# Input laid out by numpy: x and the output transposed, parameter vectors as columns, w_ada summed along rows

## The chip, the cores and the metric

The kernel runs on one core of a Trainium2 chip. TensorE (PE in the profile) multiplies matrices; VectorE (DVE), ScalarE (ACT) and GpSimd (POOL) do the elementwise work; SyncE (SP) issues most of the transfers, and a second queue is ScalarE's. The measure is the time of one execution on the device in microseconds, as a median of several runs.

## The reference

x is 512 tokens of 1024 features; 16 meta tokens are put in front, so 528 tokens pass through the first block. It has two layers, then a norm; the second block has one layer whose norms are modulated by a vector c.

```python
for l in range(2):                       # first block
    u = rms_norm(h, ln_mix[l])
    (aq, ..., gz) = split_in(u @ w_in[l])
    y_a = windowed_sink_attention(...)   # y_b: axial rope, y_c: differential, y_d: gated linear attention
    merged = sum(gate[n] * (y_n @ w_branch[l, n]))
    h = h + merged @ w_out[l]
    u = rms_norm(h, ln_ffn[l])
    h = h + (silu(u @ w_ffn_gate[l]) * (u @ w_ffn_up[l])) @ w_ffn_down[l]
x = rms_norm(h, ln_final)[:, META_END:]

mod = silu(c) @ w_ada + b_ada            # second block: 1024 -> 9 x 1024
sh1, sc1, ga1, sh2, sc2, ga2, sh3, sc3, ga3 = split(mod, 9)
h = rms_norm(x, g_pre_ff1) * (1 + sc1) + sh1
x = x + 0.5 * ga1 * rms_norm(swiglu(h, ...), g_post_ff1)
# mixer: sliding-window attention and a state space model, with sh2, sc2, ga2
# a second swiglu with sh3, sc3, ga3
```

## The kernel before

The activations stay transposed in SBUF: eight tiles h[k] of 128 features by 528 tokens. Every product is in fp32 precision made of three matmuls of rounded operands (mm3, L258 to L260): high by high, low by high, high by low. A weight tile arrives through SP's queue in a raw tile `wr` (L215, L217), ScalarE rounds it to its high half (L218), VectorE subtracts for the low half (L219). The tokens are worked on in two halves, (0, 272) and (272, 528), or without the meta tokens (16, 272) and (272, 528).

A norm squares the tiles on ScalarE (L86), sums the squares over the features by matmuls against a column of ones (L97, one per 128 tokens and tile), computes the reciprocal root on VectorE (L107, L268 to L275), spreads it over the partitions by TensorE (L112, L115), copies that as a row to SBUF (L116, L117), and scales and splits the tiles (L345, L230, L231).

load_x (L363) brings x in as four tiles of 128 tokens by 1024 features, transposes the 128x128 blocks on TensorE (L376, L387), copies them from PSUM on VectorE (L378, L388), and stores the tiles to `hd` in DRAM (L357), from where the end of the layer reads the old h again (L353). columns (L303) brings parameter vectors as rows into a `stage` tile with a transfer each on ScalarE's queue (L311, L315), transposes them (L321) and copies them as columns (L323). ada (L1834) is called 72 times in between other work: for 128 outputs it loads two pieces of w_ada of 128x4x128 (L1840) into `ho`, a pool of two tiles, adds up the eight products with c on VectorE (L1844, L1846), sums over the partitions by a matmul with ones (L1848), and adds b_ada (L1849). The last norm of the second block scales (L2238) and adds the old x (L2241); out (L2613) then transposes each half to tokens by features (L2623), copies it from PSUM (L2624), and stores it (L2626).

A class Plan at the end of the file takes all instructions and draws an order for every engine, SP's queue among them, by a list scheduler with costs and priorities, and fixes it by dependencies. So the text of the program doesn't give the order, and any change in the work draws a new one for all engines.

Of the kernel before, what the change touches and what calls it, by code (L numbers as in the profile page):

```python
# [119 lines left out]
class Net:  # L120
# [35 lines left out]
    def small(self, w, tag, bufs=None):  # L156
        self.n += 1
        if w > 32:
            return self.sp.tile([P, 128], F32, tag="wide", name=f"{tag}_{self.n}", bufs=2)[:, :w]
        if w > 8:  # L160
            return self.sp.tile([P, 32], F32, tag="mid", name=f"{tag}_{self.n}", bufs=6)[:, :w]
        return self.sp.tile([P, 8], F32, tag="tiny", name=f"{tag}_{self.n}", bufs=56)[:, :w]
# [115 lines left out]
    def setup(self):  # L278
        nc, cp, I = self.nc, self.cp, self.ins
        o = self.offs["rest"][0]  # L280
        self.misc = cp.tile([P, self.offs["total"][0]], F32, tag="misc", name="misc")
# [3 lines left out]
        self.hd = self.dp.tile([KC, P, NT], F32, tag="hd", name="hd")  # L285
        self.lo_engs = [nc.vector]
# [6 lines left out]
    def setup_rest(self):  # L293
        nc, I = self.nc, self.ins
        o = self.offs["rest"][0]
        nc.scalar.dma_start(self.misc[:, o:], I["c_misc"][:, o:])
# [5 lines left out]
    def columns(self, groups):  # L302

        nc = self.nc
        rows, where = 0, {}
        st = self.small(P, "stage", bufs=2)
        for keys, ap, wide in groups:
            nl = len(keys)
            if wide:
                n = ap.shape[1] // P  # L310
                nc.scalar.dma_start(st[rows:rows + nl * n, :], ap.rearrange("l (a b) -> (l a) b", b=P))  # L311
            else:
                n = 1
                for s in range(2):
                    nc.scalar.dma_start(st[rows:rows + nl, 64 * s:64 * s + 64], ap)  # L315
            for k in keys:
                where[k] = (rows, n)
                rows += n
        self.n += 1
        ps = self.pst("t")  # L320
        nc.tensor.transpose(ps[:, :rows], st[:rows, :], self.ident[:rows, :rows])  # L321
        col = self.cp.tile([P, rows], F32, tag=f"col{self.n}", name=f"col{self.n}")
        nc.vector.tensor_copy(col, ps[:, :rows])  # L323
        self.col.update({k: col[:, r:r + n] for k, (r, n) in where.items()})
# [38 lines left out]
    def load_x(self):  # L363
        nc, I = self.nc, self.ins
        with self.pool("xin", "R") as xp:
            mt = xp.tile([NM, 1024], F32, name="mt")
            nc.scalar.dma_start(mt, I["meta_tokens"])
# [3 lines left out]
            self.columns([([f"ln_mix{l}" for l in range(2)], I["ln_mix"], True)])  # L371
            self.ahead = [self.wload(w, KC) for w in self.qk_columns(0, 512)]
            self.h = [self.xtile("hn") for _ in range(KC)]
            pm = self.pst("t")
            for k in range(KC):
                nc.tensor.transpose(pm[:, k * NM:(k + 1) * NM], mt[:, k * P:(k + 1) * P], self.ident[:NM, :NM])  # L376
            for k in range(KC):
                nc.vector.tensor_copy(self.h[k][:, 0:NM], pm[:, k * NM:(k + 1) * NM])  # L378
            sq = self.squares()
            norm = None  # L380
            for i, (a, b) in enumerate(self.halves(0)):
                for k in range(0, KC, 2):
                    ps = self.pst("mm")
                    for j in range(2):
                        for t in range(2):
                            o = (2 * j + t) * P
                            nc.tensor.transpose(ps[:, o:o + P], xt[2 * i + t][:, (k + j) * P:(k + j + 1) * P], self.ident)  # L387
                        nc.vector.tensor_copy(self.h[k + j][:, NM + 256 * i:b], ps[:, 256 * j:256 * j + 256])  # L388
                        sq.add(self.h[k + j], a, b)
                norm = norm or self.norm(sq, self.h, self.col["ln_mix0"], 0)  # L390
                norm(i)
            for k in range(KC):
                self.store_h(k, 0)
# [75 lines left out]
    def params1(self):  # L469
        nc, I = self.nc, self.ins  # L470
        cp = self.cp
        two = lambda n: [f"{n}{l}" for l in range(2)]
        self.columns([(two("ln_ffn"), I["ln_ffn"], True), (["ln_final"], I["ln_final"][None, :], True)] + self.params2_names())
        g = [(["b_ada"], I["b_ada_2"], True)] if "b_ada_2" in I else []
        self.columns(g + [(two("qn"), I["qk_norm_q"], False), (two("kn"), I["qk_norm_k"], False),
                          (two("sub"), I["diff_subnorm"], False), (two("hout"), I["hgrn_out_norm"], False)])
        self.sink, self.sinkM, self.nlam = [], [], []
        self.gq = []
        for l in range(2):
# [8 lines left out]
            d = self.small(128, "lam", bufs=2)  # L488
            nc.scalar.dma_start(d, I["diff_lambda"][l:l + 1].rearrange("a b c -> a (b c)").to_broadcast([P, 128]))
            dv = d.rearrange("p (a b c) -> p a b c", a=2, b=2)  # L490
            pr = self.small(64, "lamp", bufs=2)
# [85 lines left out]

# [1216 lines left out]


CM = 3


class Parts:

# [1294 lines left out]
```

## Time and profile before

| | us |
|---|---|
| median of 3 runs | 3288.27 |
| lowest, highest | 3285.03, 3296.5 |
| profiled execution | 3297.02 |
| its span in the trace | 3295.2 |
| TensorE busy | 3096.8 (94%) |
| TensorE weight loads busy | 2717.5 (82%) |
| VectorE busy | 1857.9 (56%) |
| ScalarE busy | 1277.6 (39%) |
| GpSimd busy | 418.2 (13%) |

The mean granted clock of TensorE was 0.962 of full speed. The profile lists, for the engines by line, how long they were busy and what ended their idle time; a weight load (PEld) runs beside the matmul before it. A line number is that of the kernel; a helper's line gathers the work of all its callers.

### The profile page before, as it was taken

To read this page: it belongs to the slowest core of one execution; us is meant where nothing else is said; L and a number is where in the kernel's file an instruction comes from. 1 tells how busy PE (TensorE), PEld (TensorE's weight loads), DVE (VectorE), ACT (ScalarE), POOL (GpSimd) and SP (SyncE) were. 2 spreads that over 40 slices of the span, in tenths; PEclk is the share of its full clock that TensorE was granted. 3 is DMA by queue.
4 is the path that set the end of the run, shared out by engine and by line. 5 is a ranking of instruction groups with operands and counts; after the bars stand their busy time and mean duration, and the time that the engine had idled before them with its cause. 6 is when DMAs were issued, how large, how long until landed. Compare 5 with 4: busy or idle time off the path is not lost. (4 is left out here: it accounts for less than half of the span.)

```text
span 3295.2 us, 57803 instructions
## 1 busy us (share of the span) xinstructions
PE 3096.8 (94%) x21892; PEld 2717.5 (82%) x21892; DVE 1857.9 (56%) x5063; ACT 1277.6 (39%) x2856; POOL 418.2 (13%) x444
## 2 busy tenths in 40 slices
PE   7888999999999978899999999999999998899997
PEld 6777888999999977777678878789888987888887
DVE  4466588744645857567975464864222655732224
ACT  2356444333232245564434322243232535433332
POOL 1101000002110011020001111421110111211101
PEclk9899999999999988899999999989999999889998
DMA  4721223343544673022344354574333565133342
GB/s 139 178 51 45 73 73 95 103 126 112 157 122 120 172 169 67 27 79 81 93 134 142 112 150 133 166 222 121 93 96 111 147 187 152 53 109 96 92 124 93
DMA packets 645883, 380.41 MB, mean 115 GB/s; under 512 B 66500, under 2 KB 613884, under 8 KB 645476
## 3 DMA queue, kind: packets, MB, share of 16 engines
q1 hardware_dynamic: 628520, 365.22, 38.0%
q0 software_dynamic: 13632, 9.61, 2.0%
q8 instruction: 172, 2.82, 0.4%
q10 hardware_dynamic: 3452, 1.89, 0.2%
q14 instruction: 107, 0.88, 0.1%
HBM read 333.16 MB, written 45.52 MB: 115 GB/s over the span
## 5 line engine op out<-in xcount | busy, mean ns | idle before, releaser
L258 PE MATMUL ps_mm<-u,wh 128*128 128x256 f32 (+2 forms) x2928 | 970.8, 333 | 19.6 <-ACT g L1514 4.2
L260 PE MATMUL ps_mm<-u,wh 128*128 128x256 f32 (+2 forms) x2928 | 961.9, 330 | 0.3 <-DVE u L231 0.2
L259 PE MATMUL ps_mm<-u,wh 128*128 128x256 f32 (+2 forms) x2912 | 955.9, 330 | 4.6 <-DVE wh L219 4.6
L258 PEld LDWEIGHTS ps_mm<-u,wh 128*128 128x128 f32 x2928 | 563.1, 193 | 77.3 <-issue 12.0
L218 ACT ACTIVATE wh<-wr 128x512 fp32r<-128x512 f32 (+1 forms) x588 | 354.5, 619 | 690.9 <-PE ps_mm L259 261.7
L219 DVE TENSOR_TENSOR wh<-wr,wh 128x512 fp32r<-128x512 f32 (+1 forms) x531 | 367.5, 704 | 450.1 <-issue 231.3
L259 PEld LDWEIGHTS ps_mm<-u,wh 128*128 128x128 f32 x2912 | 560.3, 193 | 53.3 <-DVE wh L219 5.5
L260 PEld LDWEIGHTS ps_mm<-u,wh 128*128 128x128 f32 x2928 | 562.1, 193 | 50.9 <-issue 4.7
L259 PE MATMUL ps_mm<-hid,wh 128*128 128x256 f32 (+2 forms) x988 | 299.1, 311 | 3.4 <-DVE wh L219 3.4
L258 PE MATMUL ps_mm<-hid,wh 128*128 128x256 f32 (+2 forms) x948 | 287.7, 312 | 2.7 <-ACT wh L218 2.7
L260 PE MATMUL ps_mm<-hid,wh 128*128 128x256 f32 (+2 forms) x948 | 287.4, 311 | 0.0
L1846 DVE SCALAR_TENSOR_TENSOR acc<-ho,cact,acc 128x128 f32<-128x128 f32 x504 | 186.6, 374 | 40.0 <-DMA ho<-in_w_ada_dram 32.5
L259 PEld LDWEIGHTS ps_mm<-hid,wh 128*128 128x128 f32 x988 | 185.1, 191 | 15.8 <-DVE wh L219 4.6
L258 PEld LDWEIGHTS ps_mm<-hid,wh 128*128 128x128 f32 x948 | 178.0, 191 | 13.2 <-ACT wh L218 2.9
L260 PEld LDWEIGHTS ps_mm<-hid,wh 128*128 128x128 f32 x948 | 178.0, 191 | 9.7 <-issue 0.4
L231 POOL TENSOR_TENSOR hid<-g,hid 128x512 fp32r<-128x512 f32 (+1 forms) x85 | 92.4, 1087 | 684.6 <-ACT hid L230 684.6
L218 ACT ACTIVATE wh<-wrx 128x512 fp32r<-128x512 f32 (+1 forms) x160 | 96.0, 601 | 205.5 <-PE ps_mm L260 100.6
L219 DVE TENSOR_TENSOR wh<-wrx,wh 128x512 fp32r<-128x512 f32 (+1 forms) x131 | 87.4, 668 | 136.5 <-issue 115.8
L88 POOL TENSOR_TENSOR na<-na,g 128x256 f32<-128x256 f32 (+2 forms) x62 | 63.4, 1022 | 771.6 <-issue 418.2
L258 PE MATMUL ps_mm<-u,hid 128*128 128x256 f32 (+1 forms) x448 | 133.3, 298 | 16.1 <-ACT hid L218 16.0
L259 PE MATMUL ps_mm<-u,hid 128*128 128x256 f32 (+1 forms) x448 | 133.6, 298 | 5.2 <-DVE hid L219 5.1
L260 PE MATMUL ps_mm<-u,hid 128*128 128x256 f32 (+1 forms) x448 | 132.5, 296 | 0.0
(591 smaller groups left out, 5575.9 us busy)
## 6 DMA issues: line engine op xcount, KB each, us to landing
wr<-in_w_in_dram SPq DMA_DIRECT2D x220, 256.0 KB
ho<-in_w_ada_dram SPq DMA_DIRECT2D x144, 256.0 KB
wr<-in_w_ffn_down_dram SPq DMA_DIRECT2D x80, 256.0 KB
wr<-in_w_down_dram SPq DMA_DIRECT2D x66, 256.0 KB
wr<-in_w_ffn_gate_dram SPq DMA_DIRECT2D x62, 256.0 KB
wr<-in_w_gate_dram SPq DMA_DIRECT2D x61, 256.0 KB
wr<-in_w_ffn_up_dram SPq DMA_DIRECT2D x60, 256.0 KB
wr<-in_w_up_dram SPq DMA_DIRECT2D x60, 256.0 KB
```

The costliest lines, as they stand in the source:

```text
L88: nc.gpsimd.tensor_tensor(out=acc[:, a:b], in0=acc[:, a:b], in1=sq[:, a:b], op=ALU.add)
L218: self.last_split = nc.scalar.activation(hi[:, i:e], raw, AF.Copy)
L219: (nc.vector if o else eng).tensor_tensor(out=lo[:, i:e], in0=raw, in1=hi[:, i:e].bitcast(F32), op=ALU.subtract)
L231: (eng or self.nc.vector).tensor_tensor(out=lo, in0=x, in1=hi.bitcast(F32), op=ALU.subtract)
L258: T.matmul(o, lhsT=wh, rhs=xh[:, a:b], start=start, stop=False)
L259: T.matmul(o, lhsT=wl, rhs=xh[:, a:b], start=False, stop=False)
L260: T.matmul(o, lhsT=wh, rhs=xl[:, a:b], start=False, stop=stop)
L1846: V.scalar_tensor_tensor(out=acc, in0=w[:, k], scalar=c, in1=acc, op0=ALU.mult, op1=ALU.add)
```

## The change

The sizes of the work on activations and the weight matrices' loads are untouched. Numpy hands over some inputs in another order, before the launch, and turns the output after it.

```diff
 def load_x(self):
-    xt = [xp.tile([P, 1024], F32, tag="xt", name=f"xt{b}", bufs=4) for b in range(4)]
-    for b in range(4):
-        nc.sync.dma_start(xt[b], I["x"][0, b * P:(b + 1) * P, :])
...
-                    nc.tensor.transpose(ps[:, o:o + P], xt[2 * i + t][:, (k + j) * P:(k + j + 1) * P], self.ident)
-                nc.vector.tensor_copy(self.h[k + j][:, NM + 256 * i:b], ps[:, 256 * j:256 * j + 256])
...
-    for k in range(KC):
-        self.store_h(k, 0)
+    self.columns(True)
+    for a, b in self.halves(0):
+        for k in range(KC):
+            nc.sync.dma_start(self.h[k][:, a:b], I["c_x"][k][:, a:b])
+        if a == 0:
+            self.ahead = [self.wload(w, KC) for w in self.qk_columns(0, 512)]
...
 def old_h(self, f, a, b=NT):
-    self.nc.sync.dma_start(t[:, a:b], self.hd[f][:, a:b])
+    self.nc.sync.dma_start(t[:, a:b], self.hsrc[f][:, a:b])
...
 def columns(self, first):
+    self.nc.scalar.dma_start(self.cols[:, t], ap[:, t])
...
 def ada(self, g):
-    ws = [self.xtile("ho")[:, :512].rearrange("p (k f) -> p k f", k=4) for _ in range(2)]
...
-                V.scalar_tensor_tensor(out=acc, in0=w[:, k], scalar=c, in1=acc, op0=ALU.mult, op1=ALU.add)
-    nc.tensor.matmul(ps[:, 0:1], lhsT=acc, rhs=self.ones[:, 0:1], start=True, stop=True)
-    V.tensor_tensor(out=self.mod[:, g:g + 1], in0=ps[:, 0:1], in1=self.col["b_ada"][:, g:g + 1], op=ALU.add)
+    for e in range(2):
+        w = self.xtile("ho")[:, :512]
+        self.nc.sync.dma_start(w, self.ins["c_ada"][g, e])
+        self.nc.vector.tensor_tensor_reduce(out=w, in0=w, in1=self.cact, scale=1.0, scalar=0.0, op0=ALU.mult, op1=ALU.add,
+                                            accum_out=self.mod[:, 72 * e + g:72 * e + g + 1])
...
 def ada_end(self):
+        self.nc.sync.dma_start(b, self.ins["c_bada"][:, 24 * i:24 * i + 24])
+        for e in range(2):
+            self.nc.tensor.matmul(ps[64 * e:64 * e + 64, :24], lhsT=self.const("fold"),
+                                  rhs=self.mod[:, 72 * e + 24 * i:72 * e + 24 * i + 24],
+                                  start=True, stop=True, tile_position=(0, 64 * e), skip_group_check=True)
+        V.tensor_tensor(out=m, in0=ps[:, :24], in1=b, op=ALU.add)
...
 def half(n):
-                    nc.tensor.transpose(ps[:, k * P:(k + 1) * P], f[4 * i + k][:, a + b * P:a + (b + 1) * P], self.ident)
-                (nc.vector.tensor_copy if i else nc.scalar.copy)(o[:, :512], ps)
-                nc.sync.dma_start(self.outs["out"][0][t:t + P, 512 * i:512 * (i + 1)], o[:, :512])
+            nc.sync.dma_start(self.outs["out"][k][:, 256 * n:256 * n + 256], f[k][:, a:a + 256])
...
-    mk = self.misc[:, o + QOFF[m]:o + QOFF[m] + n2]
+    mk = self.qmask[:, QOFF[m]:QOFF[m] + n2]
...
+def laid_out(inputs):
+    tokens = np.concatenate([a["meta_tokens"], a["x"][0]], 0)
+    return {"c_x": tokens.T.reshape(KC, P, NT), "c_cols": np.concatenate([columns_of(a, n, w) for n, w in VECTORS], 1),
+            "c_bada": columns_of(a, "b_ada_2", False),
+            "c_ada": a["w_ada_2"][0].T.reshape(72, 2, 64, 2, 512).transpose(0, 1, 3, 2, 4).reshape(72, 2, P, 512)}
```

old_h reads c_x until the first layer's new h is stored, and `hd` from then on; columns is called twice, with one load each. The lines with `mk` are masked_q's; the rope's `perm` is handled alike, and SP loads both tables once a layer. In c_ada one output's 1024 weights stand along two rows of 512 on partitions p and p + 64, so a piece has 64 outputs; c, made silu on ScalarE and VectorE, is spread over the partitions as 128x512, and the `fold` matmuls add the two partitions of an output. The pool tag "wide" is gone, "tiny" has 52 tiles for 56.

The planner's order moves at the places where work goes. TensorE at the start, before: transposes of the second half (L387, `xt`) and the sums of its squares (L97) stand among the first products (L258, L259).

```order
L387 MATMUL ps_mm_344<-misc,xt_86 128x128
L258 MATMUL ps_mm_586<-u_225,wh_97 128x272
L259 MATMUL ps_mm_586<-u_225,wh_98 128x272
L97 MATMUL ps_q_304<-misc,g_310 128x1 x2
L387 MATMUL ps_mm_344<-misc,xt_85 128x128
L387 MATMUL ps_mm_344<-misc,xt_86 128x128
L97 MATMUL ps_q_304<-misc,g_318 128x1 x2
```

The third matmul of the first product comes only after more transposes and sums, eleven rows on.

TensorE at the start, in the changed kernel: the sums of the first half (L97), the broadcast (L112, L115), and the first products (L256 to L258).

```order
L97 MATMUL ps_q_156<-misc,g_190 128x1 x3
L112 MATMUL ps_t_214<-misc,nr_198 128x128 x2
L115 MATMUL ps_t_214<-misc,nr_198 128x16
L256 MATMUL ps_mm_470<-u_138,wh_96 128x272
L257 MATMUL ps_mm_470<-u_138,wh_97 128x272
L258 MATMUL ps_mm_470<-u_139,wh_96 128x272
L256 MATMUL ps_mm_470<-u_140,wh_96 128x272
```

The transposes are gone from it, and the first products follow the broadcast at once.

TensorE at the end, before: the last product of the first half (L258 to L260 with `ps_mm_34674`), the sums (L97), the broadcast (L112), the transposes of the output (L2623, nine of them in a row), and then the second half's products.

```order
L258 MATMUL ps_mm_34674<-hid_33851,wh_34664 128x256
L259 MATMUL ps_mm_34674<-hid_33851,wh_34665 128x256
L260 MATMUL ps_mm_34674<-hid_33852,wh_34664 128x256
L97 MATMUL ps_q_34745<-misc,na_31883 128x1 x2
L97 MATMUL ps_q_34745<-misc,g_34743 128x1 x2
L112 MATMUL ps_t_34769<-misc,nr_34753 128x128 x2
L2623 MATMUL ps_mm_34790<-misc,hn_34029 128x128
L2623 MATMUL ps_mm_34790<-misc,hn_34129 128x128
```

The second half's first product (`ps_mm_34821`) comes behind the last of these transposes.

TensorE at the end, in the changed kernel: the sums (L97) and then products of the second half (`ps_mm_34090`). The broadcast (L112) stands 66 matmuls later.

```order
L256 MATMUL ps_mm_33989<-hid_33043,wh_33856 128x256
L257 MATMUL ps_mm_33989<-hid_33043,wh_33857 128x256
L258 MATMUL ps_mm_33989<-hid_33044,wh_33856 128x256
L97 MATMUL ps_q_33937<-misc,na_31075 128x1 x2
L97 MATMUL ps_q_33937<-misc,g_33935 128x1 x2
L256 MATMUL ps_mm_34090<-hid_31076,wh_34060 128x256
L257 MATMUL ps_mm_34090<-hid_31076,wh_34061 128x256
L258 MATMUL ps_mm_34090<-hid_31077,wh_34060 128x256
```

The broadcast, which needs VectorE's result, no longer stands right behind the sums.

SP's queue in the first layer's last part, before: pieces of w_ada (L1840, `ho`) between weight loads (L217, `wr`).

```order
L217 DMA wr_19310<-in_w_branch_dram 128x2x128
L1840 DMA ho_18796<-in_w_ada_dram 128x4x128
L1840 DMA ho_18797<-in_w_ada_dram 128x4x128
L217 DMA wr_19316<-in_w_in_dram 128x4x128
L217 DMA wr_19320<-in_w_in_dram 128x4x128
L217 DMA wr_19410<-in_w_branch_dram 128x2x128
L1840 DMA ho_19032<-in_w_ada_dram 128x4x128
L217 DMA wr_19416<-in_w_in_dram 128x4x128
L217 DMA wr_19420<-in_w_in_dram 128x4x128
L1840 DMA ho_19033<-in_w_ada_dram 128x4x128
L217 DMA wr_19531<-in_w_branch_dram 128x2x128
```

One or two pieces stand between two or three weight loads here.

SP's queue about there, in the changed kernel: the pieces (L1827) stand in runs, between weight loads (L215) and the load of the mask table (L1181).

```order
L1827 DMA ho_17884<-in_c_ada_dram 128x512
L215 DMA wr_17550<-in_w_in_dram 128x4x128
L215 DMA wr_17623<-in_w_branch_dram 128x2x128
L1827 DMA ho_17887<-in_c_ada_dram 128x512
L1827 DMA ho_18095<-in_c_ada_dram 128x512
L1827 DMA ho_18098<-in_c_ada_dram 128x512
L1827 DMA ho_18290<-in_c_ada_dram 128x512
L1827 DMA ho_18293<-in_c_ada_dram 128x512
L215 DMA wr_17629<-in_w_in_dram 128x4x128
L1181 DMA qmask<-in_c_qmask_dram 128x62
L215 DMA wr_17633<-in_w_in_dram 128x4x128
L215 DMA wr_17729<-in_w_branch_dram 128x2x128
```

Five pieces now stand in a row before the next weight load.

Over the whole queue, three or more pieces of w_ada stand in a row at 26 places (16 runs of three, 7 of four, 3 of five), where before it was 4 (1 of three, 2 of four, 1 of five). On TensorE 17609 rows of the order become 17472, on VectorE 4783 become 4561, on ScalarE 2654 become 2642, and on SP 1454 become 1471.

## Rows read from the trace of the kernel before

**Rows 1.** The page: busy us, share and instructions of each engine.

```profile
PE 3096.8 (94%) x21892; PEld 2717.5 (82%) x21892; DVE 1857.9 (56%) x5063; ACT 1277.6 (39%) x2856; POOL 418.2 (13%) x444
```

**Rows 2.** Forty slices, two of them: busy us (instructions), granted clock, DMA share, GB/s.

```profile
411.90:494.30 82.40, 82.17 (x994) 73.94 (x996) 67.57 (x145) 37.95 (x102) 5.11 (x10) 1.00 0.25 73
...
1977.10:2059.50 82.40, 82.40 (x367) 67.12 (x366) 37.50 (x83) 20.54 (x36) 11.03 (x8) 1.00 0.45 133
```

**Rows 3.** Timeline of the start: start us, us, engine, line, operation, count, [idle before].

```profile
7.56 6.16 SPq L215 DMA_DIRECT2D wr<-in_w_in_dram  x8
...
23.43 0.16 DVE L107 TENSOR_SCALAR nv<-ps_q 128x3 f32<-128x3 f32 x1 [5.76 <-PE ps_q L97]
...
23.58 0.61 ACT L218 ACTIVATE wh<-wr 128x512 fp32r<-128x512 f32 x1
...
27.56 0.16 DVE L275 SCALAR_TENSOR_TENSOR nr<-rt,ry 128x3 f32<-128x3 f32 x1
...
29.39 0.38 ACT L117 COPY g<-ps_t 128x256 f32<-128x256 f32 x1
...
37.75 0.57 PE L258 MATMUL ps_mm<-u,wh 128*128 128x272 f32 x1
...
39.51 5.12 PE L97 MATMUL ps_q<-misc,g 128*128 128x1 f32 x24
...
44.49 0.57 PE L260 MATMUL ps_mm<-u,wh 128*128 128x272 f32 x1
```

**Rows 4.** Slices of 5 us at the start.

```profile
5.00:10.00 5.00, 1.73 (x11) 1.32 (x11) 0.86 (x8) 0.72 (x1) 0.00 (x0) 1.00 1.05 319
```

**Rows 5.** Timeline of TensorE at one of the w_ada sums.

```profile
2052.47 0.39 PE L259 MATMUL ps_mm<-u,wh 128*128 128x512 f32 x1
2052.70 0.39 PE L260 MATMUL ps_mm<-u,wh 128*128 128x512 f32 x1
2052.92 0.28 PE L1848 MATMUL ps_t<-misc,acc 128*128 128x1 f32 x2
...
2053.38 0.39 PE L259 MATMUL ps_mm<-u,wh 128*128 128x512 f32 x1
```

**Rows 6.** Line L1846: who waited for it (us, times).

```profile
  PE ps_t L1848: 6.4, 8
```

**Rows 7.** Costliest groups of the page: busy us, mean ns, idle before, releaser.

```profile
L1846 DVE SCALAR_TENSOR_TENSOR acc<-ho,cact,acc 128x128 f32<-128x128 f32 x504 | 186.6, 374 | 40.0 <-DMA ho<-in_w_ada_dram 32.5
```

**Rows 8.** Lines L1335 and L1096 on VectorE: ns min/median/max.

```profile
L1335 DVE TENSOR_TENSOR d<-U,off x32: 671/684/693, 377.8 to 1625.5; 128x512 f32<-128x512 f32 x32
...
L1096 DVE DVE_READ_ACCUMULATOR2_ANT tmC<- x64: 75/83/87, 164.9 to 1355.7; 128x1 f32 x64
```

**Rows 9.** Timeline of the end.

```profile
3231.29 0.61 PE L97 MATMUL ps_q<-misc,g 128*128 128x1 f32 x4 [0.63 <-ACT g L86]
...
3234.38 0.71 PE L112 MATMUL ps_t<-misc,nr 128*128 128x128 f32 x4 [2.49 <-DVE nr L275]
...
3241.51 1.76 PE L2623 MATMUL ps_mm<-misc,hn 128*128 128x128 f32 x7 [0.18 <-DVE hn L2241]
...
3242.91 0.56 PE L258 MATMUL ps_mm<-hid,wh 128*128 128x256 f32 x1
...
3288.09 0.74 DVE L2241 TENSOR_TENSOR hn<-hn,u 128x256 f32<-128x256 f32 x2
...
3288.23 3.25 PE L2623 MATMUL ps_mm<-misc,hn 128*128 128x128 f32 x14 [0.18 <-DVE hn L2241]
...
3291.51 0.69 DVE L2624 COPY u<-ps_mm 128x512 f32<-128x512 f32 x1 [1.02 <-PE ps_mm L2623]
```

**Rows 10.** Two slices after the last gap, with the granted clock.

```profile
3242.84:3245.80 2.96, 2.96 (x15) 2.96 (x15) 0.69 (x1) 0.00 (x0) 0.00 (x0) 0.50 0.41 153
3245.80:3250.00 4.20, 4.20 (x38) 4.20 (x36) 1.29 (x2) 1.15 (x2) 0.00 (x0) 0.99 0.23 72
```

**Rows 11.** Waits of SP's queue: us in total, times, longest us.

```profile
SPq L1840 <- DVE acc L1846: 179.0, 103, 7.5
```

More of the change, by code (lines that the diff above doesn't have):

```diff
@@ L280, in setup @@
         o = self.offs["rest"][0]
[L281 removed]
+        self.misc = cp.tile([P, self.offs["total"][0] + 8], F32, tag="misc", name="misc")
         nc.sync.dma_start(self.misc[:, :o], I["c_misc"][:, :o])
@@ L300, in setup_rest, with columns @@
         nc.gpsimd.tensor_copy(self.mask.rearrange("p a b -> p (a b)"), t)
[L302 to L324, printed above, removed]
+    def columns(self, first):
+        ap, n = self.ins["c_cols"], COLS["ln_mix"][1]
+        if first:
+            self.cols = self.cp.tile([P, ap.shape[1]], F32, tag="cols", name="cols")
+        t = slice(0, n) if first else slice(n, ap.shape[1])
+        self.nc.scalar.dma_start(self.cols[:, t], ap[:, t])
+        self.col = {k: self.cols[:, o:o + w] for k, (o, w) in COLS.items()}
+        self.col["ln_mix0"], self.col["ln_mix1"] = (self.cols[:, KC * l:KC * l + KC] for l in range(2))
     def token_blocks(self, c0):
@@ L471, in params1 @@
         cp = self.cp
[L472 to L476, printed above, removed]
+        self.columns(False)
         self.sink, self.sinkM, self.nlam = [], [], []
@@ L940, in branch_B @@
                 nc.sync.dma_start(rope[a], self.ins["c_rope"][:, NT * a:NT * (a + 1)])
+            self.n += 1
+            perm = pool.tile([P, P], F32, tag="perm", name=f"perm_{self.n}")
+            nc.sync.dma_start(perm, self.ins["c_perm"])
             xs = [(x3[0], cq, 0), (x3[1], cq, 0), (x3[2], 0, 1)]
@@ L1213, in branch_D @@
         sg = [y[:, c] for c in range(2)]
+        self.qmask = pool.tile([P, 62], F32, tag="qmask", name="qmask")
+        nc.sync.dma_start(self.qmask, self.ins["c_qmask"])
         for h in range(4):
@@ L1547, in emit @@
                 self.store_h(f, c0)
-        norm = []
+                stored.append(f)
+                if len(stored) == KC:
+                    self.hsrc = self.hd
+        norm, stored = [], []
         def mid(i):
@@ new lines, in ada_begin @@
+        self.mod = self.cp.tile([P, 144], F32, tag="mod", name="mod")
+        t = self.xtile("na")[:, :512]
+        self.cact = self.cp.tile([P, 512], F32, tag="cact", name="cact")
+        for i in range(2):
+            nc.scalar.dma_start(self.cact[64 * i:64 * i + 64], self.ins["c_2"][:, 512 * i:512 * i + 512].to_broadcast([64, 512]))
+        nc.scalar.activation(t, self.cact, AF.Tanh, scale=0.5)
+        V.tensor_scalar(out=t, in0=t, scalar1=1.0, scalar2=0.5, op0=ALU.add, op1=ALU.mult)
+        V.tensor_tensor(out=self.cact, in0=t, in1=self.cact, op=ALU.mult)
```

106 lines of the change are left out of this document (44 added, 62 removed).

## Prediction

> **What bounds the kernel now.** I read the totals by engine first, then the span in forty slices, then four close-ups: the start, one place among the w_ada sums, the queue waits, and the end. TensorE is busy 3096.8 of 3295.2 us, VectorE 1857.9 [rows 1]. The reader is to see that the rest, 198.4 us, isn't spread evenly: in the stretch where w_ada is summed TensorE shows 82.17 and 82.40 busy of 82.4 us [rows 2], so there an instruction taken out of TensorE's stream is worth its whole step, and VectorE's 67.57 and 37.50 us in the same slices lie beside it. At the start and at the end TensorE stands still for other engines. The change touches these three places, so the sum has three terms, on the profiled execution's own time, 3297.0 us (span 3295.2). That execution is 8.8 us above the median of the runs, 3288.3; I take the gain from the profile and subtract it from the median.
>
> **Start.** Now TensorE turns four x tiles round, VectorE copies the pieces out, and the sums of the first norm come between; they reach VectorE at 23.43 us. From there to its result are 4.3 us (27.56 and 0.16 more, four weight splits lying between), to the end of the row copy on ScalarE 2.05 us more (29.39 and 0.38), and then 8.0 us pass until the first product at 37.75, since TensorE stands in order behind transposes of the second half that wait for VectorE. Then the second half's sums follow, and only at 44.49 does the stream of products begin [rows 3]. In the changed kernel all transposes and copies go; the first half's sums are 24 matmuls, each two records in the trace, and 24 records take 5.12 us [rows 3], so 48 take 10.2 us. The eight pieces of x's first half (139 KB each) and the small table are 1.18 MB, 3.7 us at the 319 GB/s that the start shows [rows 4]; the first piece and its square should be there by about 6 us, so the sums end at 16. Adding the same 4.3 and 2.05 gives a row copy done at 22.4 (against 29.77), and it stands behind six weight splits on ScalarE, of which the last ended at 24.2 before [rows 3] because ScalarE first issues some thirty loads of parameter rows; now these are two. One scale and two split steps, 2 us, give a first product at 24.5. The second half's 32 records are 6.8 us inside the stream, so what was reached at 44.49 is reached at 31.3: 13 us gained. Bounds: 5 us, if the pieces land late (second rival); 18, if the sums go at the 0.15 us a record of the end (four in 0.61 [rows 9]). I take 13.
>
> **The sums of w_ada.** Removed from TensorE are 72 matmuls of one column (L1848). Where one stands in the stream, the distance from L260 at 2052.70 to the L259 after next at 2053.38 is 0.68 us, with one L258 between; two ordinary steps are 2 x 0.235 (2052.47 to 2052.70) [rows 5]. So one costs 0.22 us, 72 cost 15.8. TensorE waited 6.4 us more for VectorE's sums before them [rows 6]. Added are 6 folding matmuls, 1.3 us. Term: 15.8 + 6.4 - 1.3 = 21, which I round to 20 since a few stand where TensorE was idle anyway; bounds 8 (a slice where it waits for something else) and 24. On VectorE 504 steps took 186.6 us, 0.374 each [rows 7]. Instead come 144 row sums over 512 columns, which no row shows. From below there is one such step of a quarter of the width; nearest is a plain product of two 128x512 operands, 0.684 us, with the reading of an accumulator, 0.083 us [rows 8]: 0.77 us each, 110 us in all; were it double, 220 us, it would be somewhat more than what goes. Either way it lies beside a TensorE that is busy, so I cost VectorE's relief at nothing; the cover is gone only if weight splits queue behind these sums (third rival).
>
> **End.** After the last product of the first half TensorE does the norm's sums (until 3231.90), waits for VectorE, broadcasts, waits again for the eight scalings, transposes, and starts the next product at 3242.91 [rows 9]: 11.0 us without a product. In the changed order two sum rows are followed at once by products of the second half, 66 of them before the broadcast, 7.3 us at 0.111, more than the 2.5 us that VectorE's chain needs. The gap closes but for the broadcast's 0.5: 10.5 us. After the pause the granted clock is 0.50, the 1.2 GHz level, for 2.96 us with 15 products, then 0.99 with 38 in 4.20 us [rows 10]; 15 x (0.197 - 0.111) = 1.3 us fall away with the pause. The seven transposes left of the first half, later in the stream, are between 0.8 us, at the product's 0.111, and 1.6, at the 0.232 of fourteen in 3.25 us [rows 9]; I take 1.2. At the very end the last scaled tile is there at 3288.83 (3288.09 and 0.74); 14 transposes and four copies last until 3292.20 [rows 9], and then a store is issued and lands. A store straight from the tile spares 3.4 us, less 0.4 for one more issue in SP's queue: 3.0. Term: 10.5 + 1.3 + 1.2 + 3.0 = 16. Bounds: 11, if the second half's weights are split too late to be multiplied at once; 18, if the stores cost nothing.
>
> **The rest, at nothing.** The parameter table replaces some thirty small loads on ScalarE's queue, counted in the start. The permutation and mask tables become four small loads on SP, each ahead of its user; a queue step of 0.77 us at the start (eight in 6.16) [rows 3] puts them at 3 us in all if nothing hides them, and the weights loaded in advance should. The tiles named tiny fall from 56 to 52, read only in the norms' chains. The planner draws all engines anew: of the 198.4 us in which TensorE is idle it may win or lose a tenth, 20 us either way, and I take zero.
>
> Sum: 13 + 20 + 16 = 49. Profile 3297.0 - 49 = 3248; on the median 3288.3 - 49 = **3239 us**.
>
> **Rivals.** *A. The w_ada matmuls were hidden.* A busy TensorE needn't be at its peak: weight loads are busy 73.94 and 67.12 us in the two slices, so 8 to 15 us of each 82 are not the array's own [rows 2]. If single matmuls filled such holes, only 13 + 16 = 29 is won: 3259. Against it stands the shift of 0.22 us in rows 5. The Trainium skill ("Perfetto Trace Analysis", Identifying the Most-Contended Engine) speaks for this rival: matmul busy share is a poor measure, and the busy share of weight loads a better one; by it TensorE would be at 82%, not 94%. The shift seen in the stream speaks against its use here. Chance 0.2.
>
> *B. The start is bound by many small transfers.* SP issued eight 256 KB loads in 6.16 us, one per 0.77 [rows 3]. If that is the price of any load, the sixteen pieces of x take 12.3 us, and the first weights are issued at 13.9 in place of 7.56, with the splits and the row copy behind them: 6 us later, a start worth about 7 us, 3245. By the Trainium skill ("DMA: Bandwidth & Descriptors", Bandwidth) a 64 KB transfer reaches 138 GB/s and one of 1 MB 341; an estimate by the lower figure puts the first half's 1.18 MB at 8.6 us. The 319 GB/s of rows 4 were seen with four 512 KB pieces in flight, so they don't decide it. Chance 0.1.
>
> *C. Slower: VectorE waits for its own w_ada loads.* These loads use a pool of two tiles. In the new order of SP's queue 26 runs of three to five of them stand between weight loads, where before there were four such runs; together they hold 39 loads beyond the second of a run. Each must wait for a tile to be summed, and holds back the weights queued behind it on SP; on VectorE the sum that waits for it holds back the weights' lower halves. Before, VectorE waited 32.5 us for such loads at L1846 [rows 7], and SP 179.0 us in 103 waits of up to 7.5 us for VectorE [rows 11], without TensorE seeing it. If each of the 39 costs TensorE 1.25 us, the 49 us are gone; from 1.5 us on it is slower, and at 1.8 us it would be 3288 + 70 - 49 = 3309. Weights are loaded ahead in this stretch, and TensorE's busy share there says that they came in time. Chance 0.06.
>
> *D. The new order is better throughout.* With less on VectorE, TensorE waits less for it in other stages too: a tenth of 198.4 us more gained, 3219. Chance 0.1.
>
> **How the numbers follow.** The forecast has 0.54: 3239, with a range of its own of 3224 to 3256 from the bounds of its terms. A measurement of this kernel tells 0.3%, about 10 us, from no change. Forecast, A, B and D lie clear of that: faster 0.92; the tails of A and C that end within 10 us: same 0.04; C beyond it: slower 0.04. The range that is to hold 8 in 10 reaches from D's middle to beyond A: 3212 to 3268.
>
> **What would show it.** Right: first product near 24.5 us and the stream unbroken from about 31; no transposes of x or of the output; one row sum with its read near 0.77 us; under 1 us between the last norm's sums and the next product, at the full granted clock; the stretch of w_ada shorter by about 20 us with TensorE as busy. Wrong: TensorE idle before L257, whose operand is the lower half of a weight, in the w_ada stretch (C); the same length of that stretch without the matmuls (A); the first weight splits after 16 us (B). If the gain is under 25 us, the end or the w_ada term is mis-sized, since the start alone can't carry that.

## The result, and the profile after

The changed kernel takes 3248.8 us (median of 4, 3247.4 to 3251.4) where the kernel before takes 3292.4 (median of 4, 3285.0 to 3298.3): the ratio is 0.9871, 95% interval 0.9855 to 0.9888, or 37 to 48 us gained. Its profiled execution takes 3251.4 us with a span of 3249.3, so the two profiles are 45.9 us apart.

The page's engine totals of the changed kernel, against [rows 1]:

```profile
PE 3061.7 (94%) x21685; PEld 2677.3 (82%) x21685; DVE 1764.4 (54%) x4675; ACT 1274.8 (39%) x2853; POOL 427.3 (13%) x444
```

TensorE is busy for 35.1 us less, VectorE for 93.5. What is left idle on TensorE fell by only 10.8 us, from 198.4 to 187.6: most of the gain is work taken out of a stream that was full. In the slice where TensorE was busy throughout [rows 2], it still is, by the changed kernel's own time, which is some 24 us ahead in the work there:

```profile
1977.10:2059.50 82.40, 82.02 (x370) 64.38 (x369) 38.50 (x53) 21.63 (x38) 20.75 (x14) 1.00 0.38 119
```

The timeline of its start, to be read beside [rows 3]:

```profile
10.75 5.19 SPq L213 DMA_DIRECT2D wr<-in_w_in_dram  x8
...
11.37 6.56 PE L97 MATMUL ps_q<-misc,g 128*128 128x1 f32 x30 [0.41 <-ACT g L86]
...
17.96 0.16 DVE L107 TENSOR_SCALAR nv<-ps_q 128x3 f32<-128x3 f32 x1 [7.66 <-PE ps_q L97]
...
22.23 0.16 DVE L273 SCALAR_TENSOR_TENSOR nr<-rt,ry 128x3 f32<-128x3 f32 x1
...
24.97 0.63 ACT L216 ACTIVATE wh<-wr 128x512 fp32r<-128x512 f32 x1 [1.70 <-DMA wr<-in_w_in_dram]
...
25.55 0.38 ACT L117 COPY g<-ps_t 128x256 f32<-128x256 f32 x1
...
27.25 0.59 PE L256 MATMUL ps_mm<-u,wh 128*128 128x272 f32 x1 [3.34 <-ACT u L228]
...
33.77 3.09 PE L97 MATMUL ps_q<-misc,g 128*128 128x1 f32 x24
...
36.72 0.57 PE L258 MATMUL ps_mm<-u,wh 128*128 128x272 f32 x1
```

The sums reach VectorE at 17.96 (before 23.43), the row copy ends at 25.93 (29.77), and the first product is at 27.25 (37.75). The stretch from there to 33.77 holds 25 products, where before there were two ahead of the last sums. The row copy still stands behind the sixth weight split, and that one waits for its load.

The new row sum, in the answer on its line and in the page's costliest groups, and SP's waits at it, against [rows 7], [rows 8] and [rows 11]:

```profile
L1828 DVE CUSTOM_DVE_ANT_0 ho<-ho,cact x144: 674/692/1806, 345.5 to 1932.4; 128x512 f32<-128x512 f32 x144
L1828 DVE DVE_READ_ACCUMULATOR2_ANT mod<- x144: 70/82/88, 346.1 to 1933.1; 128x1 f32 x144
```

```profile
L1828 DVE CUSTOM_DVE_ANT_0 ho<-ho,cact 128x512 f32<-128x512 f32 x144 | 105.7, 744 | 114.5 <-DMA ho<-in_c_ada_dram 114.3
```

```profile
SPq L1827 <- DVE mod L1828: 153.0, 116, 4.8
```

One sum takes 0.692 us and its read 0.082, together 0.774. The 0.692 is the median; the page's mean is 0.744. VectorE waits 114.3 us for the loads, where before it waited 49.5 (32.5 at L1846 and 17.0 at L1844, which [rows 7] doesn't hold).

The timeline and the slices at the end, against [rows 9] and [rows 10]:

```profile
3209.25 0.58 PE L97 MATMUL ps_q<-misc,g 128*128 128x1 f32 x4
...
3217.56 0.61 PE L112 MATMUL ps_t<-misc,nr 128*128 128x128 f32 x4
...
3245.34 0.74 DVE L2228 TENSOR_TENSOR hn<-hn,u 128x256 f32<-128x256 f32 x2
```

```profile
3190.00:3233.00 43.00, 43.00 (x367) 43.00 (x366) 22.29 (x47) 14.35 (x31) 6.71 (x8) 1.00 0.42 126
```

The sums and the broadcast are 8.3 us apart with products between them, TensorE is busy for all of 43 us at the full granted clock, and the span ends 3.2 us after the last scaled tile (3246.08), where it took 6.4.

**Where the time came from.** I took, for a set of TensorE's lines, the first or last start that the answer on the line gives, in each trace, and subtracted the one of before (us; a time of before stands at the head):

| kernel | 147 | 319 | 387 | 435 | 635 | 1054 | 1446 | 2058 | 2650 | 3278 |
|---|---|---|---|---|---|---|---|---|---|---|
| changed | -14.2 | -11.9 | -6.8 | -2.4 | -9.3 | -16.0 | -16.7 | -24.5 | -29.1 | -42.8 |
| the end alone | -0.9 | 0.1 | 0.7 | 0.7 | 0.7 | 2.2 | -2.4 | -3.7 | -9.3 | -23.4 |
| start alone | -11.2 | -7.6 | -5.3 | -5.4 | -7.3 | -5.3 | -7.1 | -12.6 | -17.1 | -17.8 |
| all but w_ada | -12.9 | -9.8 | -7.9 | -8.1 | -8.5 | -7.0 | -11.0 | -14.2 | -12.5 | -29.4 |
| four tiles | -13.4 | -10.3 | -3.1 | 1.7 | -3.8 | -10.1 | -7.6 | -15.5 | -19.3 | -33.5 |
| sums spread | -13.4 | -11.2 | -6.2 | -4.5 | -11.3 | -20.2 | -19.2 | -32.6 | -34.6 | -51.1 |
| no column matmuls | 3.5 | 4.0 | 3.8 | 5.8 | 9.0 | 4.5 | 2.1 | -7.2 | -8.6 | -11.8 |
| 72 more matmuls | -13.1 | -9.5 | -3.3 | 1.5 | -2.2 | -3.1 | -3.5 | -10.4 | -13.5 | -28.8 |

The kernels below the first row are those of the experiments. The start's 13 us are there at 147; half of it is lost by 387, and so it is in the start alone, and why stays open; a further 4.4 goes by 435; the two feed-forwards of the first block (635 to 1054, 1446 to 2058) bring 6.7 and 7.8, of which 3.2 in the second come without the w_ada change too; 4.6 come from 2058 to 2650, where the work wasn't changed; the end brings 13.7, and 3.2 more behind the last column of the table.

### The profile page after: what moved, and what is told of

It is laid out like the page before. It is cut to its first block, busy times and chain, and to the rows that moved or that the text cites. A ratio compares the mean times of both kernels' runs of the same rounds, so it can differ in the third digit from the quotient of the medians.

```text
span 3249.3 us, 57071 instructions
## 1 busy us (share of the span) xinstructions
PE 3061.7 (94%) x21685; PEld 2677.3 (82%) x21685; DVE 1764.4 (54%) x4675; ACT 1274.8 (39%) x2853; POOL 427.3 (13%) x444
## 4 chain that ended last, share of the span: by engine, by line
PE 53%; DVE 4%; DMA 3%; ACT 2%; issue 1%; SPq 1%; POOL 0%; DVEq 0%; ACTq 0%; POOLq 0%
PE ps_mm L256 16%; PE ps_mm L257 15%; PE ps_mm L258 15%; PE ps_q L97 1%; PE ps_o L748 1%; PE ps_t L706 1%; DMA wr<-in_w_in_dram 1%; DMA ho<-in_c_ada_dram 1%; DVE wh L217 1%; ACT wh L216 0%; DVE hn L2225 0%; PE ps_t L2128 0%; PE ps_o L2462 0%; PE ps_s L2427 0%; DVE u L1877 0%
## 5 line engine op out<-in xcount | busy, mean ns | idle before, releaser
L256 PE MATMUL ps_mm<-u,wh 128*128 128x256 f32 (+2 forms) x2928 | 970.1, 333 | 31.7 <-ACT u L228 6.7
L258 PE MATMUL ps_mm<-u,wh 128*128 128x256 f32 (+2 forms) x2928 | 959.8, 329 | 0.1
L256 PEld LDWEIGHTS ps_mm<-u,wh 128*128 128x128 f32 x2928 | 562.5, 193 | 96.2 <-issue 12.9
L217 DVE TENSOR_TENSOR wh<-wr,wh 128x512 fp32r<-128x512 f32 (+1 forms) x531 | 370.2, 710 | 430.7 <-issue 236.9
L258 PEld LDWEIGHTS ps_mm<-u,wh 128*128 128x128 f32 x2928 | 562.5, 193 | 50.0 <-issue 4.3
L256 PE MATMUL ps_mm<-hid,wh 128*128 128x256 f32 (+2 forms) x948 | 285.1, 310 | 3.3 <-ACT wh L216 3.3
L258 PE MATMUL ps_mm<-hid,wh 128*128 128x256 f32 (+2 forms) x948 | 285.7, 310 | 0.0
L256 PEld LDWEIGHTS ps_mm<-hid,wh 128*128 128x128 f32 x948 | 176.1, 189 | 13.7 <-ACT wh L216 3.4
L258 PEld LDWEIGHTS ps_mm<-hid,wh 128*128 128x128 f32 x948 | 176.1, 189 | 9.7 <-issue 0.4
L1828 DVE CUSTOM_DVE_ANT_0 ho<-ho,cact 128x512 f32<-128x512 f32 x144 | 105.7, 744 | 114.5 <-DMA ho<-in_c_ada_dram 114.3
L217 DVE TENSOR_TENSOR wh<-wrx,wh 128x512 fp32r<-128x512 f32 (+1 forms) x131 | 86.1, 658 | 149.7 <-issue 130.4
L256 PE MATMUL ps_mm<-u,hid 128*128 128x256 f32 (+1 forms) x448 | 134.5, 300 | 18.4 <-ACT hid L216 18.4
L258 PE MATMUL ps_mm<-u,hid 128*128 128x256 f32 (+1 forms) x448 | 132.6, 296 | 0.0
```

Source lines behind the costliest of these rows:

```text
L217: (nc.vector if o else eng).tensor_tensor(out=lo[:, i:e], in0=raw, in1=hi[:, i:e].bitcast(F32), op=ALU.subtract)
L256: T.matmul(o, lhsT=wh, rhs=xh[:, a:b], start=start, stop=False)
L258: T.matmul(o, lhsT=wh, rhs=xl[:, a:b], start=False, stop=stop)
L1828: self.nc.vector.tensor_tensor_reduce(out=w, in0=w, in1=self.cact, scale=1.0, scalar=0.0, op0=ALU.mult, op1=ALU.add, accum_out=self.mod[:, ...
```

## The experiments

**The parts, one at a time.** Four kernels take the change apart: the end alone, all but w_ada, all but the end, and the start alone (with the parameter table and the pools).

```diff
 # the end alone: the kernel before, with
...
-                        nc.tensor.transpose(ps[:, k * P:(k + 1) * P], f[4 * i + k][:, a + b * P:a + (b + 1) * P], self.ident)
...
+                    nc.sync.dma_start(self.outs["out"][k][:, 256 * n:256 * n + 256], f[k][:, a:a + 256])
 # all but w_ada: the changed kernel, with ada_begin, ada and ada_end of before
 # all but the end: the changed kernel, with half of before
 # the start alone: the changed kernel, with all of these of before
```

> The kernel before with the transposed output alone. Theory (the end is a sum of its own): the 11.0 us without a product close, the two slow-clock and transpose terms and the last copies go, 16 us gained, about 3274 for a before of 3290. Rival (a new order anywhere moves the time by as much as the change does): anything from 3260 to 3310, with the two traces apart long before the last feed-forward. In the trace, up to the last feed-forward, less than 3 us of shift by the theory.

> The changed kernel with the sums of w_ada as they were (column by column, 72 matmuls with ones). Theory: start and end remain, 13 + 16 = 29 us gained, about 3261 for a before of 3290, 14 to 20 us above the changed kernel. Rival A (the w_ada matmuls were hidden): as fast as the changed kernel, 3249 within 5.

> The changed kernel with the output transposed on TensorE as before. Theory: it loses the end's 16 us, about 3265. Rival (half of the end's gain came from VectorE being freer, or the gap closes by the new order even with the transposes): 3257 or less.

> The changed kernel with both the w_ada sums and the transposed end as before: the new start, the parameter table and the pools alone. Theory (parts add up: all but w_ada gained 28, the end alone 20): 8 us gained, 3284 for a before of 3292, with 13 us of shift in the trace near 150 us and 8 near 390. Rival (the start's 13 us carry to the end): 3279 or less. Rival (two parts share a gain): 3288 or more.

Measured: the end alone 3271.7 us (ratio 0.994, 0.9917 to 0.9963: 20 gained, 12 to 27); all but w_ada 3264.6 (0.9915, 0.9893 to 0.9938: 28 gained); all but the end 3268.0 (0.9927, 0.9902 to 0.9952: 24 gained); the start alone 3279.5 (0.9953, 0.9936 to 0.997: 15 gained, 10 to 21). So w_ada is worth 15.8 us by what is lost without it, the end 20 by itself and 19.2 by its loss, the start 15 by itself. They add up to about 50 where 43 is seen; each of these has an interval of 5 us or more to either side, so I don't read a loss into the difference. Against rival A, the kernel without the w_ada change isn't as fast as the changed one. The expectation of 8 us for the start alone missed, 15 were measured. The traces don't show these 15 as the start's own: of 11.2 us at 147 there are 5.4 left at 435, and 10.0 come from 1446 to 2650 (table), where the end alone gains 6.9 too, in the order of before.

The end alone shows something else. Its order on TensorE is that of before, row for row, up to the end, so a change in the work doesn't always draw a new one; and yet its trace is 9.3 us ahead at 2650 us (table). Of this, 6.1 us arise in one stretch. The rows hold the same instructions in both traces, the kernel before first:

```profile
2150.00:2300.00 150.00, 135.11 (x1013) 131.82 (x1013) 85.30 (x186) 66.31 (x141) 33.65 (x30) 0.90 0.59 176
```

```profile
2146.40:2290.30 143.90, 132.62 (x1014) 129.25 (x1013) 85.62 (x184) 66.15 (x141) 33.13 (x30) 0.92 0.61 183
```

The kernel before is busy for 2.5 us longer, at a granted clock of 0.90 against 0.92, and idle for 3.6 us more, all of it in waits for ScalarE (11.6 against 8.0 us). Two executions of one order can differ by as much. The profiled one of before stood 4.6 us above its median and that of the end alone 1.3 below, so every value of the table after 2058 holds some us that are that execution's own; from there on the difference of two columns is to be read, not the value. From 2650 to 3278 the end alone gains 14.1, the changed kernel 13.7.

**The matmuls by themselves.** One kernel takes the 72 matmuls out of the kernel before and leaves VectorE's steps; one puts 72 like them into the changed kernel.

```diff
 # without the column matmuls: the kernel before
-        ps = self.pst("t")
-        nc.tensor.matmul(ps[:, 0:1], lhsT=acc, rhs=self.ones[:, 0:1], start=True, stop=True)
-        V.tensor_tensor(out=self.mod[:, g:g + 1], in0=ps[:, 0:1], in1=self.col["b_ada"][:, g:g + 1], op=ALU.add)
+        V.tensor_tensor(out=self.mod[:, g:g + 1], in0=acc[:, 0:1], in1=self.col["b_ada"][:, g:g + 1], op=ALU.add)
 # with 72 more: the changed kernel, at the end of ada
+        ps = self.pst("t")
+        self.nc.tensor.matmul(ps[:, 0:1], lhsT=self.ident, rhs=self.mod[:, 72 + g:73 + g], start=True, stop=True)
```

> The kernel before without the 72 matmuls that sum w_ada over the partitions; each partition's own partial sum stands in their place, so mod is not the full sum. VectorE's steps stay. Theory: TensorE's 72 steps of 0.22 us and 6.4 us of waits go, about 20 us, 3270 for a before of 3290. Rival A (they filled holes): no change, 3290 within 5. If the gain is 20 here and in the run without the w_ada change the loss is smaller, VectorE's row sums give part of it back.

> The changed kernel with 72 more one-column matmuls on TensorE, each on a sum that VectorE has just made, their result unused. Theory: 72 steps of 0.22 us, 16 us slower than the changed kernel, 3265. Rival A (they fill holes): 3249 within 5. If both this and the kernel before without its 72 matmuls show 11, a matmul costs 0.15 on the mean.

Measured: without them 3281.0 us (0.9963, 0.995 to 0.9976: 12 gained, 8 to 16); with 72 more 3264.8 (0.9922, 0.9907 to 0.9937), 16.0 above the changed kernel, a difference known to some 7 us. The second is the forecast's 72 x 0.22 = 15.8, but that it meets it to the tenth is luck. Of the 13.9 us that its trace is behind the changed kernel's at the end, 3.9 are there at 435, ahead of all 72; from 635 to 1054 it loses 5.8 with 26 of them, 0.22 each, and from 1446 to 2058 only 0.9 with 35 (table). Between neighbours the price holds there too: around the one at 2044.1 us two steps of 0.236 take 0.689. The first gained less than 20: its trace is 9.0 us behind the kernel before at 635, ahead of 61 of the 72, and gains 4.5 from 635 to 1054 and 9.3 from 1446 to 2058. That the loss ahead of 635 is the other order's is likely, not shown. Neither agrees with rival A, by which both would have been zero.

**The waits for w_ada's loads.** A third and fourth tile for these loads:

```diff
-            w = self.xtile("ho")[:, :512]
+            w = self.xtile("t1" if e else "ho")[:, :512]
```

> The changed kernel with the two pieces of each w_ada sum in two tile tags, so four tiles instead of two. Theory: VectorE's 114 us of waits for these loads shrink below 60, but they lie beside TensorE's work, so the time stays at 3249 within 6. Rival C (these waits hold back weight splits and cost part of the gain): 3243 or less, with fewer waits of TensorE in 345 to 435 us.

Measured: 3263.1 us (0.9918, 0.9901 to 0.9935), 14 slower than the changed kernel, against both theories. The waits did shrink, from 114.3 to 49.9 us (35.7 in one tag and 14.2 in the other), and nothing was gained. That alone doesn't refute rival C, since the order is another one, and the waits that are left can stand where they hurt. The table shows where it lost: between 319 and 435 us, 12.0 against 9.5 for the changed kernel, and more in small steps until 1446. Why it lost 14 in all stays open; the next experiment looks at the first of these places.

**The crowd at 340 to 440 us.** In the trace of the kernel before, 14 of VectorE's narrow steps on w_ada stand in this stretch, 5.8 us; in the changed kernel 30 row sums do, and in the one with four tiles 32. The rows, first the changed kernel, then four tiles, hold only L1828 and count a sum and the read behind it as two. The 65 of 144 in the expectation below were counted that way; they are 32 sums.

```profile
340.00:440.00 100.00, 20.98 (x60) 0.98 0.49 147
```

```profile
340.00:440.00 100.00, 22.31 (x64) 0.97 0.50 151
```

The same time holds the gated linear attention, whose work on VectorE TensorE waits for. The waits of TensorE and VectorE from 387 to 435 us in the changed kernel, and one place among them:

```profile
PE ps_mm L256 <- DVE hn L1485: 2.0, 3, 1.4
...
DVE ho L1828 <- DMA ho<-in_c_ada_dram: 15.6, 6, 4.5
```

```profile
406.29 0.69 DVE L1828 CUSTOM_DVE_ANT_0 ho<-ho,cact 128x512 f32<-128x512 f32 x1 [4.55 <-DMA ho<-in_c_ada_dram]
...
408.15 0.43 DVE L1485 SCALAR_TENSOR_TENSOR hn<-g,ps_mm 128x272 f32<-128x272 f32 x1
...
408.63 0.40 PE L256 MATMUL ps_mm<-u,wh 128*128 128x272 f32 x1 [1.39 <-DVE hn L1485]
```

A row sum waits 4.55 us for its load. In VectorE's order a second sum, a weight split and L1485, which reads a PSUM tile, stand behind it, and TensorE's next product into such a tile waits 1.39 us for L1485. This is rival C's mechanism, a sum that waits for its load and holds back what is behind it, only with L1485 in the place of a weight's lower half. In all six traces with 30 to 32 sums in the stretch (changed, all but the end, four tiles, 72 more, two queues in both executions) TensorE waits 1.4 to 2.6 us for L1485 there; before, in the start alone, all but w_ada, and the two with the sums spread it doesn't. With four tiles the waits for loads fall to 6.4 us there, but two of the three left (2.84 and 3.22 us) stand ahead of an L1485, and TensorE still waits 2.6.

The test ties each row sum to the weight split that stands before it in the program, so that they stay near their place, and raises the calls in each feed-forward from 28 to 33:

```diff
-            self.spare(1 if f % 4 else 2)
+            self.spare(1 if f % 2 else 2)
...
+            if self.eng[n] == 2 and any(t.startswith("wh") for t in tiles):
+                last = n
+            if self.eng[n] == 2 and any(t.startswith("mod_") for t in tiles) and any(t.startswith("ho_") for t in tiles):
...
+                self.edge(n, last, False)
```

> The changed kernel with each row sum of w_ada ordered on VectorE behind the weight split that stands before it in the program, and the calls in each feed-forward raised from 28 to 33, so that they spread over the feed-forward instead of crowding into 340 to 480 us (65 of 144 stand there now). Theory (the crowd delays VectorE's work for the gated linear attention, and TensorE loses about 5 us there): the shift against the kernel before at 435 us goes from -2.4 to -7 or below, and the time to 3244. Rival (that loss is the luck of an order and comes back elsewhere): 3249 within 4, with the loss at another place.

Measured: 3242.1 us (0.9845, 0.9829 to 0.9862), 6.7 below the changed kernel; the intervals of the two ratios overlap at their ends. Between 340 and 440 us there are 8 row sums left. TensorE's busy time from 320 to 440 us in four kernels, each from its own trace: all but w_ada, sums spread, changed, four tiles.

```profile
320.00:440.00 120.00, 117.91 (x1088) 105.36 (x1089) 75.39 (x236) 55.99 (x155) 5.92 (x15) 0.99 0.24 70
```

```profile
320.00:440.00 120.00, 116.65 (x1065) 103.40 (x1065) 71.06 (x223) 56.24 (x153) 5.21 (x15) 0.97 0.26 76
```

```profile
320.00:440.00 120.00, 114.60 (x1026) 100.25 (x1024) 84.24 (x265) 56.16 (x153) 7.71 (x15) 0.99 0.42 124
```

```profile
320.00:440.00 120.00, 112.84 (x955) 100.04 (x954) 81.53 (x261) 55.59 (x153) 6.68 (x15) 0.96 0.41 126
```

The more row sums in the stretch, the less TensorE is busy: 117.91, 116.65, 114.60, 112.84 for 17 narrow steps, 8, 30 and 32 row sums. From 387 to 435 nothing is lost without the w_ada change, 1.7 us with the sums spread, 4.4 changed and 4.8 with four tiles (table). About 2 us of each of these losses is work that was drawn into the stretch: in the changed kernel TensorE is busy for 50.59 of the 53.0 us (380 to 433), with the sums spread for 50.28 of 50.4, before for 48.17 of 48.4. So its idle time grows by 2.2 us there, and that this hangs on the crowd is shown, by the waits and by the five kernels without it. In the test the loads moved with the sums, so it doesn't part the sums' own time from the waits for their loads. That spreading the sums gains 6.7 at the end is only likely: the shift at 435 was -4.5, not the -7 expected, most of the rest came later, and beside x on two queues the same edit gains 3.2, within the intervals.

**The start on two queues.**

```diff
-                nc.sync.dma_start(self.h[k][:, a:b], I["c_x"][k][:, a:b])
+                (nc.scalar if a else nc.sync).dma_start(self.h[k][:, a:b], I["c_x"][k][:, a:b])
```

> The changed kernel with the second halves of x issued from ScalarE's queue instead of SP's, so that SP comes to the first weights eight loads earlier (10.75 us now). Theory (rival B in part: the start is held by SP's queue, weights landing late, and the row copy behind the splits that wait for them): first weight load before 7 us, last of the six splits before 22 (24.97 now), first product near 24.5 in place of 27.25. Rival (the pieces of x themselves land too slowly, the squares set the sums at 17.96): the first product stays within 1 us of 27.25.

> The changed kernel with the second halves of x on ScalarE's queue, as before, timed. Theory (the start is only 0.6 us earlier at the first product, so the 3243.5 of the single run is the rest of the order): 3244 to 3250. Rival B: the shorter start carries to the end, 3244 or less in every run.

> Both edits: row sums spread and x on two queues. Theory: 3240, the sum of the two. Rival (each edit only draws another order): anything from 3238 to 3255, not the sum.

The timeline of the first execution:

```profile
5.76 7.19 SPq L213 DMA_DIRECT2D wr<-in_w_in_dram  x8
...
17.64 0.15 DVE L107 TENSOR_SCALAR nv<-ps_q 128x3 f32<-128x3 f32 x1
...
21.77 0.63 ACT L216 ACTIVATE wh<-wr 128x512 fp32r<-128x512 f32 x1 [1.88 <-DMA wr<-in_w_in_dram]
...
22.43 0.69 DVE L217 TENSOR_TENSOR wh<-wr,wh 128x512 fp32r<-128x512 f32 x1 [1.36 <-ACT wh L216]
...
23.43 0.16 DVE L273 SCALAR_TENSOR_TENSOR nr<-rt,ry 128x3 f32<-128x3 f32 x1
...
26.70 0.60 PE L256 MATMUL ps_mm<-u,wh 128*128 128x272 f32 x1 [1.59 <-ACT u L228]
```

The weights are issued 5 us earlier, the last of the six splits comes at 21.77 (24.97), as expected, and the first product comes 0.55 us earlier. The sums still arrive at 17.64, and the norm's result even later, for a weight split now stands in its chain on VectorE (22.43) whose weight waits for its load until 21.77. So an earlier issue from SP's queue isn't enough: the weights' landing still holds the first product, and the expected 24.5 missed. The time was 3243.5 in one execution, and 3257.0 in four on another chip (0.989, 0.9875 to 0.9905), of the same kernel; the kernel before took 3293.0 and 3295.6 on the two. So both expectations for the four missed. Both edits together gave 3253.8 (0.9878, 0.9864 to 0.9893), not the sum of two gains; on the same chip the spread sums alone took 3242.1, so beside them the second queue costs 11.7.

The two profiled executions of the one kernel have the same order on TensorE, and one is 11.3 us longer. 3.0 us of it arise in this stretch of the same 539 matmuls, the shorter execution first:

```profile
550.10:600.00 49.90, 49.90 (x539) 40.56 (x538) 33.47 (x72) 19.94 (x52) 0.00 (x0) 1.00 0.20 56
```

```profile
550.94:603.88 52.94, 52.94 (x539) 42.74 (x538) 33.49 (x72) 20.06 (x52) 0.00 (x0) 0.94 0.19 53
```

TensorE is busy throughout in both, at a granted clock of 1.00 and 0.94. In the longer one the clock was 0.66 from 551 to 560 us, though TensorE had been busy for 50.6 of the 51 us before.

**The part that I costed at nothing.** The kernel before with both tables in pools and 52 small tiles:

```diff
-        mk = self.misc[:, o + QOFF[m]:o + QOFF[m] + n2]
+        mk = self.qmask[:, QOFF[m]:QOFF[m] + n2]
```

> The kernel before with the permutation and the mask table loaded into pools and 52 small tiles for 56, nothing else. Theory: no change, 3292 within 8. Rival (four more loads in SP's queue and another order cost or win): over 3300 or under 3284.

Measured: 3296.3 us, ratio 1.0016 (1.0001 to 1.003): within the expected 8, and 0.3 to 10 us slower, around the 3 us that four loads in SP's queue were put at if nothing hid them. It is too small to say whether it is the loads or another order.

## Why the prediction was right

The forecast was 49 us, 43 was measured, with 49 just outside the interval of 37 to 48. The bounds of the three terms taken together give 3228 to 3264, not the 3224 to 3256 that it names as its own range. By its steps:

- *Start, 13.* The shift at 147 us is 14.2. But the steps came out otherwise: the sums at 17.96, not 16, since the first of them starts at 6.96 in place of 6, the 48 records take 10.6 us and TensorE waits 0.4 us for a square; the row copy at 25.93, not 22.4, since it stands behind a split that waits for its load; the first product at 27.25, not 24.5. What made up for it is that 25 products now stand ahead of the second half's last sums, where I had the stream begin only after them. Nor is the stream unbroken from 31 us: at 60 us TensorE waits 4.0 us for another load. And the gain doesn't last: of the changed kernel's 14.2 us 6.8 are left at 387, of the start alone's 11.2 5.4 at 435, which no step of the forecast allowed for. That the start alone still measured 15 (10 to 21) at the end is in part luck, as its trace gains 10.0 from 1446 to 2650. Rival B holds in part: the sixteen pieces and the table took SP from 0.73 to 10.70 us, 0.59 a load. Slices of 5 us of the changed kernel's start:

```profile
0.00:5.00 5.00, 0.00 (x0) 0.00 (x0) 0.00 (x0) 0.00 (x0) 0.20 (x4) 1.00 0.65 155
5.00:10.00 5.00, 3.04 (x15) 3.05 (x15) 0.15 (x3) 2.46 (x4) 0.00 (x0) 1.00 0.95 252
```

  Data moved at 155 and 252 GB/s, below the 319 that I used. The Trainium skill ("DMA: Bandwidth & Descriptors", Bandwidth) has 138 GB/s at 64 KB and 341 at 1 MB, for loads issued from GpSimd. Pieces of 139 KB, issued from SP and several under way at once, came between its two figures, so the trace agrees as far as the two can be compared.
- *w_ada, 20.* Measured 15.8, known to some 9 us. By the traces, from 435 to 2058 the changed kernel gains 22.1 us and all but w_ada 6.1, so 16.0 are w_ada's there; at 435 the changed kernel is 5.7 behind, so 10.3 of it are left when the last sum is done. The rest of the 15.8 comes behind that, where no w_ada work stands, and isn't explained. The price of a matmul in the stream was about right (16.0 for 72, unevenly by stage); that the 6.4 us of waits went too, no run shows by itself. The step that failed is the one that costed VectorE's side at nothing, "it lies beside a TensorE that is busy". A sum's price was right (0.774 against 0.77), but I had looked at two full slices, while the planner put 30 of the 144 sums into a stretch where TensorE waits for VectorE: there its idle time grew by 2.2 us from 387 to 435, and by 3.3 in 120 us against all but w_ada. Rival C had the mechanism, sums that wait for their loads, but at a price of some 2 us in one stretch and not one for each of 39 loads; and VectorE's waits before were 49.5 us, not the 32.5 that I read at one of the two lines.
- *End, 16.* 13.7 in the stream and 3.2 behind it, 16.9 by the traces and 20 (12 to 27) by the times. No product waits between the sums and the broadcast, the granted clock stays at 1.00, the second half's weights were split in time. In the table's six kernels that have the new end, it brings 13.7 to 16.9 from 2650 to 3278, in the two that don't 0.7 and 3.2. This step was worked from one gap with known neighbours, and it was the most exact.
- *Rival A* didn't come. A one-column matmul in the stream was worth its whole step between its neighbours, while weight loads were busy for only 64 to 74 of 82 us in such slices. The Trainium skill's rule ("Perfetto Trace Analysis", Identifying the Most-Contended Engine) is about how far TensorE is from its peak; for the price of one more instruction the spacing of neighbours in the timeline [rows 5] gave the answer.
- *Rival D* isn't seen in the totals, TensorE's idle time fell by 10.8 us, about what the end alone closes.

## What to carry to other kernels

Price an instruction on a full engine by the shift of its neighbours in the timeline, not by its own duration: 0.22 us against 0.25 here, and 72 of them came to 16.0. When a step is moved to an engine with slack on the mean, look where the scheduler will put it: a list scheduler can bring optional work forward into the stage where that engine is waited for, and an instruction that waits for its load there holds back all that stands behind it. Count instructions, not records, where one operation leaves two. Before a few microseconds are explained, run the same order a second time: two executions of one order differed by 9 to 11 us here. And compare the same instructions in both traces: windows of equal time hold other work as soon as one trace is ahead.

## What the runs showed of the hardware

- The same 539 matmuls, without a pause, took 49.90 us at a granted clock of 1.00 and 52.94 at 0.94 in two executions of one kernel. Over the 44 runs of before that stand beside the experiments (3285 to 3305 us), a mean clock lower by 0.001 goes with some 2 us more (correlation -0.63); what else spreads them isn't shown.
- A row sum over 128x512 in fp32 with both operands in SBUF takes VectorE 0.692 us in the median (single ones up to 1.806), as long as the plain product (0.684), and a separate instruction of 0.082 us reads the sum.
- At the start the column of granted clock says nothing: the traces hold no record of it ahead of 32.6 us (changed) and 47.6 us (before), and the column reads 1.00 there. Up to then products of 272 columns stand 0.227 us apart (27.25 to 32.2 in the changed kernel, 44.9 to 47.1 before), nearly twice the 0.125 that follows from 48.0 before. The changed kernel has the 0.227 again from 37 us on, where the clock is recorded as 0.50 (36 to 42.8 us, 0.60 in the slice below), behind 3 us of one-column sums:

```profile
27.20:32.00 4.80, 4.75 (x21) 4.75 (x22) 4.77 (x9) 2.90 (x7) 2.63 (x3) 1.00 0.21 61
```

```profile
35.00:40.00 5.00, 5.00 (x28) 5.00 (x28) 2.01 (x13) 0.40 (x1) 0.00 (x0) 0.60 0.00 2
```
